# Reordering matmuls of two widths, bank reads against weight preparation, and a wider final norm, in a float32 Conformer layer with its MLP

## The chip, the cores and the metric

The kernel runs on one NeuronCore of one Trainium2 chip. The metric is device time in microseconds (us) of one execution, as the median over several runs. The names of the engines are those of the profile: PE is the matrix engine, PEld its loading of weights, DVE the vector engine, ACT the scalar engine, POOL the general engine GpSimd, and SP the engine whose queue issues most of the DMAs.

## The reference

One layer of a streaming encoder on 512 tokens of width 2048, all in float32: an RMS norm, a Conformer convolution module, a residual, a second RMS norm, a squared-ReLU MLP with hidden width 8192, a residual, and a last RMS norm.

```python
h = rmsnorm(x, norm1_g)
y = conformer_conv(h, ...)     # matmul 2048 -> 4096, sigmoid gate, 31-tap causal
                               # convolution, layernorm, silu, matmul 2048 -> 2048
x = x + y
h = rmsnorm(x, norm2_g)
x = x + square(relu(h @ mlp_w1)) @ mlp_w2
return rmsnorm(x, final_g)     # y = x * rsqrt(mean(x*x) + 1e-6) * g
```

## The kernel before, in words

**Float32 products from rounded halves.** Every factor is split into a high part `hi` in the rounded format (`fp32r`) and a low part `lo = x - hi`. A product is then high times high, plus the two cross terms. In the second half of the MLP, the convolution module and the last pieces these are three matmuls of 512 columns (`mm3`, L395 to L397). In the first half of the MLP the activations hold `hi` and `lo` of 256 tokens side by side in one tile `y` of 512 columns. One matmul of 512 columns with the high weights `wh` (L1114) serves two terms, and one of 256 columns with the low weights `wl` (L1115) the third.

**The MLP, first half.** It is computed by seven block products (`P1` to `P7`, a Strassen scheme on two by two blocks) for each of 32 pairs of hidden tiles (`n`, L1110). A product runs over eight `p`, each with a 512 and a 256 column matmul: 1792 of each in all. The order of products is `FIRST = P1, P5, P6, P2, P7, P3, P4`. They accumulate in PSUM banks: `P1`, `P6`, `P7`, `P4` in bank X (bank 0 or 1, alternating with `n`), `P5` and `P3` in Y, `P2` in Z. A bank is read after each product that it held, into a block of the tile `four`: by an ACT copy and a DVE add (L1122, L1123), or by two DVE adds (L1120, L1123). The next product in the bank has to wait for that read.

**The weights.** `stream` is one list of all weight chunks. `emit()` prepares the next: DMA from HBM (on SP), a sum of blocks where the scheme wants one, the cast to `wh` on ACT and the subtraction to `wl` on POOL or DVE. `chunk()` (L337) takes the next chunk and first emits up to `AHEAD` further ones. Each engine works through its queue in order, so where `chunk()` stands in the program decides what each engine's queue holds ahead of the bank reads.

**The beginning of the MLP.** The output projection of the convolution module runs in four quarters `q` of eight chunks `c` (L969). The last chunks, 6 and 7 of the last quarter, are multiplied at L990 to L996, one output tile after the other, and the evacuated tiles 12 to 15 are scaled and summed into the last two `p` of `y` (`y_sums`, `pieces`). `ahead()` makes two sums of weight blocks on POOL (`t5`, `t6`, L242). For the first pair (`n` = 0) the loop does more: further `pieces`, and `residual` transposes 12 to 15 on PE into banks that are free, whose reading (`residual_read`: ACT copies, squares and DMA) is placed by the tables `RESIDUAL` and `READ_FIRST`.

**The MLP, second half.** `seven()` (L1197) runs the same scheme for groups `g` of eight hidden tiles and two halves `q` of the columns. The last group has 14 products of twelve matmuls. `add` (L1194) reads each bank on DVE into the residual tiles `acc`. A last part without the scheme adds 512 hidden units directly.

**The final norm.** `Row` (L1256) treats 128 tokens: `piece` runs six matmuls of 512 columns and adds the bank to `acc` (DVE), squares it with a sum (ACT, L1274) and multiplies by `final_g` (POOL, L1279). `total` and `factor` turn the sums into the factor `r` (L1283 to L1291), which `scale` applies (L1296 on ACT, L1298 on DVE) ahead of the output DMA. The norm of one row stands between the pieces of the next. The last piece of the last row is cut in two of 256 columns.

## Time and profile before

| | us |
|---|---|
| median of 3 runs (lowest, highest) | 1849.67 (1848.84, 1849.75) |
| the profiled execution | 1847.88 |
| its span, first to last instruction | 1846.1 |
| PE busy | 1813.8 (98%) |
| DVE, POOL, ACT busy | 1308.6, 1254.6, 1168.1 |

The profile is one execution. Its span leaves out 1.8 us of the execution's own time. Matmuls overlap: the duration of one reaches past the start of the next, so what a matmul costs in a stream is read from one start to the next. "Idle before" is the time that an engine stood still ahead of an instruction, with what released it. POOL and DMA issue rows read in the same way.

### The profile page before, as it was taken

How to read it: one execution, taken by the hardware profiler on the slowest of the kernel's cores; microseconds unless marked ns; L12 is line 12 of the kernel's file. 1: busy time of each engine (PE TensorE's matmuls, PEld its weight loads, DVE VectorE, ACT ScalarE, POOL GpSimd, SP SyncE). 2: the span in 40 equal slices, each digit the busy share in tenths (PEclk: the TensorE clock that was granted, in tenths of full speed). 3: DMA queues.
4: the chain of work that ended last, by engine and by line, in shares of the span. 5: the costliest groups of instructions: out<-in, count | busy, mean ns of one | idle time of the engine just before them, and what ended most of it. 6: DMA issues, size and time to landing. Idle time of an engine off the chain costs nothing.

```text
span 1846.1 us, 25990 instructions
## 1 busy us (share of the span) xinstructions
PE 1813.8 (98%) x9096; PEld 1535.6 (83%) x9096; DVE 1308.6 (71%) x2200; ACT 1168.1 (63%) x1789; POOL 1254.6 (68%) x717
## 2 busy tenths in 40 slices
PE   8999999999998999999999999999999999999996
PEld 6888888998886888888888888888888888888875
DVE  6899999973348767667667667656666576666676
ACT  7444444565355666666666666657777777777774
POOL 2899989944425667767767767766666767576655
PEclk9999999999999999999999999999999999999998
DMA  8333343116333555665665665594647447475332
GB/s 292 92 92 92 104 125 110 63 40 212 114 114 109 173 212 178 209 212 178 209 212 179 209 212 179 203 357 162 248 174 302 189 176 274 157 282 203 133 127 92
DMA packets 92003, 322.89 MB, mean 175 GB/s; under 512 B 10208, under 2 KB 11872, under 8 KB 91872
## 3 DMA queue, kind: packets, MB, share of 16 engines
q1 hardware_dynamic: 70992, 259.81, 41.1%
q10 hardware_dynamic: 20880, 61.42, 8.3%
q8 instruction: 72, 1.18, 0.3%
q14 instruction: 59, 0.48, 0.1%
HBM read 256.70 MB, written 64.49 MB: 174 GB/s over the span
## 4 chain that ended last, share of the span: by engine, by line
PE 86%; DVE 10%; ACT 2%; issue 1%; DMA 0%; ACTq 0%; SPq 0%; DVEq 0%
PE mm L1114 23%; PE mm L396 14%; PE mm L395 14%; PE mm L397 14%; PE mm L1115 11%; PE mm L778 8%; DVE ax L479 4%; DVE y L924 1%; PE mm L996 1%; DVE acc L1194 0%; DVE ysums L913 0%; DVE ol L582 0%; PE ax L932 0%; DVE ax L667 0%; DVE ax L475 0%
## 5 line engine op out<-in xcount | busy, mean ns | idle before, releaser
L1114 PE MATMUL mm<-y,wh 128*128 128x512 f32 x1792 | 634.9, 399 | 3.2 <-DVE four L1123 3.2
L1115 PE MATMUL mm<-y,wl 128*128 128x256 f32 x1792 | 503.7, 281 | 0.0
L1114 PEld LDWEIGHTS mm<-y,wh 128*128 128x128 f32 x1792 | 337.3, 188 | 87.7 <-DVE four L1123 3.8
L251 POOL TENSOR_TENSOR wl<-b,wh 128x1024 fp32r<-128x1024 f32 x96 | 232.0, 2417 | 193.0 <-ACT wh L250 140.3
L219 DVE TENSOR_TENSOR wl<-b,ax 128x512 fp32r<-128x512 f32 x360 | 231.2, 684 | 172.3 <-ACT ax L218 132.1
L1115 PEld LDWEIGHTS mm<-y,wl 128*128 128x128 f32 x1792 | 339.1, 189 | 0.0
L395 PE MATMUL mm<-wh,ah 128*128 128x512 f32 x840 | 326.9, 389 | 1.2 <-DVE acc L1194 1.2
L397 PE MATMUL mm<-wh,al 128*128 128x512 f32 x840 | 326.8, 389 | 0.0
L396 PE MATMUL mm<-wl,ah 128*128 128x512 f32 x840 | 326.8, 389 | 0.0
L212 ACT CAST wh<-b 128x1024 fp32r<-128x1024 f32 x210 | 221.4, 1054 | 151.4 <-PE mm L397 149.7
L192 POOL TENSOR_TENSOR b<-b,b 128x1024 f32<-128x1024 f32 x120 | 286.7, 2411 | 44.1 <-DVE wl L219 30.3
L145 POOL TENSOR_TENSOR wl<-raw,wh 128x1024 fp32r<-128x1024 f32 x84 | 200.9, 2408 | 131.0 <-ACT wh L144 130.9
L479 DVE SCALAR_TENSOR_TENSOR ax<-u,v,ax 128x512 f32<-128x512 f32 x327 | 218.0, 748 | 0.0
L395 PE MATMUL mm<-xh,wh 128*128 128x512 f32 (+1 forms) x544 | 206.5, 380 | 5.3 <-ACT wh L144 5.2
L396 PE MATMUL mm<-xl,wh 128*128 128x512 f32 (+1 forms) x544 | 205.8, 378 | 1.0 <-DVE xl L389 1.0
L397 PE MATMUL mm<-xh,wl 128*128 128x512 f32 (+1 forms) x544 | 205.4, 378 | 0.0
L218 ACT COPY ax<-wh 128x512 f32<-128x512 f32 x360 | 199.8, 588 | 5.7
L1194 DVE SCALAR_TENSOR_TENSOR acc<-mm,shift,acc 128x512 f32<-128x512 f32 (+1 forms) x241 | 169.7, 742 | 31.0 <-PE mm L397 31.0
L395 PEld LDWEIGHTS mm<-wh,ah 128*128 128x128 f32 x840 | 157.7, 188 | 34.6 <-ACT w2h L1245 1.6
L397 PEld LDWEIGHTS mm<-wh,al 128*128 128x128 f32 x840 | 157.7, 188 | 32.6
L396 PEld LDWEIGHTS mm<-wl,ah 128*128 128x128 f32 x840 | 157.7, 188 | 32.6
L144 ACT CAST wh<-raw 128x1024 fp32r<-128x1024 f32 (+1 forms) x91 | 93.5, 1037 | 143.9 <-PE mm L396 99.1
(237 smaller groups left out, 2865.1 us busy)
## 6 DMA issues: line engine op xcount, KB each, us to landing
b<-in_w1s SPq DMA_DIRECT2D x128, 512.0 KB, 5.0
b<-in_w2s SPq DMA_DIRECT2D x120, 512.0 KB, 6.4
raw<-in_w_in SPq DMA_DIRECT2D x63, 512.0 KB, 3.8
ah<-spill SPq DMA_DIRECT2D x26, 896.0 KB, 8.4
al<-spill SPq DMA_DIRECT2D x26, 896.0 KB, 9.8
raw<-in_w_out SPq DMA_DIRECT2D x32, 512.0 KB, 3.6
spill<-sh ACTq DMA_DIRECT2D x31, 512.0 KB, 7.5
spill<-sl ACTq DMA_DIRECT2D x31, 512.0 KB, 7.5
```

Of the source, the lines that this page charges most:

```text
L145: (nc.vector if sl.stop == cut else self.eng).tensor_tensor(out=lo[:, sl], in0=raw[:, sl], in1=hi[:, sl].bitcast(F32), op=ALU.subtract)
L192: nc.gpsimd.tensor_tensor(out=raw[to, hs], in0=raw[x, hs], in1=raw[y, hs], op=ALU.subtract)
L212: nc.scalar.copy(out=hi, in_=self.s)
L218: nc.scalar.copy(out=st, in_=hi[:, sl].bitcast(F32))
L219: nc.vector.tensor_tensor(out=lo[:, sl], in0=self.s[:, sl], in1=st, op=ALU.subtract)
L251: nc.gpsimd.tensor_tensor(out=lo, in0=raw[b], in1=hi.bitcast(F32), op=ALU.subtract)
L395: nc.tensor.matmul(out=ps, lhsT=wh, rhs=xh, start=first, stop=False, **how)
L396: nc.tensor.matmul(out=ps, lhsT=wh, rhs=xl, start=False, stop=False, **how)
L397: nc.tensor.matmul(out=ps, lhsT=wl, rhs=xh, start=False, stop=last, **how)
L479: nc.vector.scalar_tensor_tensor(out=o, in0=a, scalar=w, in1=c, op0=ALU.mult, op1=ALU.add)
L1114: nc.tensor.matmul(out=x, lhsT=wh, rhs=t, start=product in OPENS and p == 0, stop=p == 7, skip_group_check=True)
L1115: nc.tensor.matmul(out=x[:, :HT], lhsT=wl, rhs=t[:, :HT], start=False, stop=p == 7, skip_group_check=True)
```

## The change

**Order of column steps.** Each product of the MLP's first half issues its eight 512 column matmuls first, then its eight 256 column ones. Nothing is added or left out.

PE, at the first product of the pair `n` = 0 (the row ahead of it belongs to the output projection). Before:

```order
L996 MATMUL mm<-vl,wh 128x512
L1114 MATMUL mm<-y,wh 128x512
L1115 MATMUL mm<-y,wl 128x256
L1114 MATMUL mm<-y,wh 128x512
L1115 MATMUL mm<-y,wl 128x256
```

After, with the first three products and the transposes (`ident`) of the residual:

```order
L1008 MATMUL mm<-vl,wh 128x512
L1121 MATMUL mm<-y,wh 128x512 x8
L1123 MATMUL mm<-y,wl 128x256 x8
L1121 MATMUL mm<-y,wh 128x512 x8
L1123 MATMUL mm<-y,wl 128x256 x8
L937 MATMUL mm<-ident,xr_3950 128x128
L937 MATMUL mm<-ident,xr_3952 128x128
```

The widths no longer alternate, and the first transposes have moved from behind the first product to behind the second.

**Bank reads ahead of weights.** For `n` = 0 and in the last group, the product takes a chunk that is already prepared (`chunk_made`), and the next one is emitted (`stream.get`) behind the bank's read. The sums and pieces for `P6` move from ahead of the loop to behind the first read, `P4`'s last piece goes earlier, and the residual's first two steps move from behind products 0 and 2 to behind 1 and 3. `residual_read` writes the squares back into their bank, and two reads share one tile.

DVE, from the last evacuation of the output projection (`xr15`) to the first two bank reads of `n` = 0 (`four`). `ysums` and `y` are the activations' sums and pieces, `ax` is a block sum for the weights of a later product. Before:

```order
L950 SCALAR_TENSOR_TENSOR xr15_3974<-mm_4781,v_91,xr15_3974 128x512
L913 TENSOR_TENSOR ysums_5234<-xs_5147 128x256
L924 TENSOR_TENSOR y_5236<-ysums_5234,y_5236 128x256
L913 TENSOR_TENSOR ysums_5234<-ysums_5234,xs_5147 128x256
L924 TENSOR_TENSOR y_5240<-ysums_5188,y_5240 128x256
L924 TENSOR_TENSOR y_5243<-ysums_5234,y_5243 128x256
L261 TENSOR_TENSOR ax_5144<-t6_5150,b11_4969 128x512
L261 TENSOR_TENSOR ax_5145<-t6_5150,b11_4969 128x512
L1123 TENSOR_TENSOR four_5304<-mm_5278,four_5304 128x256
```

After:

```order
L959 SCALAR_TENSOR_TENSOR xr15_3974<-mm_4781,v_91,xr15_3974 128x512
L918 TENSOR_TENSOR ysums_5234<-xs_5145 128x256
L929 TENSOR_TENSOR y_5236<-ysums_5234,y_5236 128x256
L1131 TENSOR_TENSOR four_5291<-mm_5271,four_5291 128x256
L918 TENSOR_TENSOR ysums_5234<-ysums_5234,xs_5145 128x256
L929 TENSOR_TENSOR y_5295<-ysums_5184,y_5295 128x256
L929 TENSOR_TENSOR y_5298<-ysums_5234,y_5298 128x256
L260 TENSOR_TENSOR ax_5142<-t6_5148,b11_5033 128x512
L260 TENSOR_TENSOR ax_5143<-t6_5148,b11_5033 128x512
```

The first bank read has moved ahead of five instructions.

**Chunks 5 to 7 of the last quarter.** Chunk 6's low part is made on DVE instead of POOL, and the loads of the MLP's first blocks are issued behind the DMAs of chunks 5 and 6.

SP, from the loads of the first pair's blocks (`b`) to the last chunk (`raw`). Before:

```order
L232 DMA b11_4969<-in_w1s 128x1024
L232 DMA b12_4971<-in_w1s 128x1024
L135 DMA raw_4975<-in_w_out 128x1024
L232 DMA b22_5031<-in_w1s 128x1024
L143 DMA raw_5035<-in_w_out 128x1024
L232 DMA b21_5084<-in_w1s 128x1024
L135 DMA raw_5088<-in_w_out 128x1024
```

After:

```order
L134 DMA raw_4971<-in_w_out 128x1024
L142 DMA raw_5029<-in_w_out 128x1024
L231 DMA b11_5033<-in_w1s 128x1024
L231 DMA b12_5035<-in_w1s 128x1024
L231 DMA b22_5037<-in_w1s 128x1024
L134 DMA raw_5086<-in_w_out 128x1024
L231 DMA b21_5150<-in_w1s 128x1024
```

Chunks 5 and 6 (`raw`) now pass the blocks `b11` to `b22`, and `b21` goes behind chunk 7.

**The final norm.** A row's squares are taken over 1024 columns, POOL multiplies only columns 0 to 1535 by `final_g` (of the last row 0 to 1023), and DVE applies `r` and `final_g` in one instruction to the rest. The last 512 entries of `final_g` lie in a PSUM bank (`g3`). The small instructions of `factor` become TENSOR_SCALAR with columns as scalars.

```diff
-                w = chunk()
+                w = chunk() if n else chunk_made()
                 for p in range(8):
-                    t = y[p, product]
-                    wh, wl = (h[:, p * P : (p + 1) * P] for h in w)
-                    nc.tensor.matmul(out=x, lhsT=wh, rhs=t, ...)
-                    nc.tensor.matmul(out=x[:, :HT], lhsT=wl, rhs=t[:, :HT], ...)
+                    nc.tensor.matmul(out=x, lhsT=w[0][:, p * P : (p + 1) * P], rhs=y[p, product], ...)
+                for p in range(8):
+                    nc.tensor.matmul(out=x[:, :HT], lhsT=w[1][:, p * P : (p + 1) * P], rhs=y[p, product][:, :HT], ...)
...
         for step, (product, hs) in enumerate(ORDER):
             if hs == halves:
                 continue
-            w = chunk()
+            w = chunk() if halves == 2 else chunk_made()
...
+            stream.get(cursor[0] - 1)
...
         def factor(self):
             nc.vector.reciprocal(out=y, in_=self.root)
-            nc.vector.scalar_tensor_tensor(out=ve, in0=y, scalar=ve, in1=y, op0=ALU.mult, op1=ALU.mult)
-            nc.vector.scalar_tensor_tensor(out=self.r, in0=ve, scalar=1.5, in1=y, op0=ALU.add, op1=ALU.mult)
+            nc.vector.tensor_scalar(out=ve, in0=y, scalar1=y, scalar2=ve, op0=ALU.mult, op1=ALU.mult)
+            nc.vector.tensor_scalar(out=self.r, in0=ve, scalar1=1.5, scalar2=y, op0=ALU.add, op1=ALU.mult)
...
+        g3 = bank("ax")
+        nc.scalar.copy(out=g3, in_=fgt[1][:, 512:])
...
+            row.piece(0, 512)
+            if before:
+                before.square(1024, 2048)
+                before.total()
+            row.piece(512, 1024)
+            if before:
+                before.gain(1024, 1536)
+                before.factor()
+            row.square(0, 1024)
+            if before:
+                before.scale(0, 1024, nc.scalar)
+            row.piece(1024, 1536)
+            if before:
+                before.scale(1536, 2048, nc.vector)
+                before.scale(1024, 1536, nc.scalar)
+            row.gain(0, 512)
+            row.gain(512, 1024)
```

More of the change, by code (lines that the diff above doesn't have):

```diff
@@ L319, in trunk @@
     for q in range(4):
-        items += [Plain(w_out[q, c], None if q == 3 and c in (5, 7) else nc.gpsimd) for c in range(0 if q else 4, 8)]
+        items += [Plain(w_out[q, c], (None if c in (5, 7) else nc.vector if c == 6 else nc.gpsimd) if q == 3 else nc.gpsimd) for c in range(0 if q else 4, 8)]
     AHEAD_AT = len(items) + 2
@@ L338, in chunk, with chunk_made @@
         got = stream.get(cursor[0])
+        cursor[0] += 1
+        return got
+    def chunk_made():
+        got = stream.made[cursor[0]]
         cursor[0] += 1
@@ L970, in trunk @@
             ps = [bank() for _ in range(4)]
-            stream.AHEAD = 3 if q < 3 else 2
+            stream.AHEAD, stream.LOAD = (3, 3) if q < 3 else (2, 0)
             for c in range(8 if q < 3 else 6):
                 w = chunk()
+                if q == 3 and c == 4:
+                    for x in items[cursor[0] + 3 :][:2]:
+                        x.load()
                 for i in range(2):
@@ L1138, in trunk @@
                 if n == 1 and i == 0:
+                    read = read()
                     gone.close()
@@ L1253, in trunk @@
         nc.scalar.dma_start(out=t, in_=fg[i * 1024 : (i + 1) * 1024].partition_broadcast(P))
-        fgt += [t[:, :512], t[:, 512:]]
+        fgt.append(t)
     class Row:
         def __init__(self, b):
-            self.b, self.xs = b, []
-            self.cols = [slice(n * 512, (n + 1) * 512) for n in range(4)]
-            if b == NTOK - 1:
-                self.cols[3:] = [slice(1536, 1792), slice(1792, D)]
+            self.b = b
             self.ss = tmp.tile([P, 5], F32, tag="st", name="ss")
-        def piece(self, i, cs):
-            b, n = self.b, cs.start // 512
-            ws = slice(cs.start - n * 512, cs.stop - n * 512)
-            ps = bank()[:, : cs.stop - cs.start]
+            self.sums = 0
@@ L1270, in piece, with square @@
+        def piece(self, start, stop):
+            b, n = self.b, start // 512
+            ws = slice(start - n * 512, stop - n * 512)
+            ps = bank()[:, : stop - start]
             for k in range(2):
                 mm3(ps, tuple(x[:, k * T + b * P :][:, :P] for x in a), tuple(x[:, k * 512 + ws.start : k * 512 + ws.stop] for x in wl2[n]), k == 0, k == 1)
-            x3 = add(b, n, ps, ws)
+            add(b, n, ps, ws)
+        def square(self, start, stop):
+            i = self.sums
+            self.sums += 1
@@ L1273, in piece @@
             sq = big.tile([P, 1024], F32, tag="rb", name="sq", bufs=8)
[L1274 to L1279 removed]
+            nc.scalar.activation(out=sq[:, : stop - start], in_=x2[self.b][:, start:stop], func=AF.Square, accum_out=self.ss[:, i : i + 1])
@@ L1281, in total, with gain @@
+        def gain(self, start, stop):
+            x3, i = x2[self.b][:, start:stop], start // 1024
+            nc.gpsimd.tensor_tensor(out=x3, in0=x3, in1=fgt[i][:, start - 1024 * i : stop - 1024 * i], op=ALU.mult)
         def total(self):
             self.t, self.root, self.y, self.ve, self.r = (tmp.tile([P, 1], F32, tag="st", name=f"r{i}") for i in range(5))
-            nc.vector.tensor_reduce(out=self.t, in_=self.ss[:, : len(self.xs)], axis=mybir.AxisListType.X, op=ALU.add)
+            nc.vector.tensor_reduce(out=self.t, in_=self.ss[:, : self.sums], axis=mybir.AxisListType.X, op=ALU.add)
@@ L1314, in trunk @@
             before = row
         before.total()
-        before.gain(i, nc.vector)
         before.factor()
-        for i in (4, 0, 3, 1, 2):
-            before.scale(i, i < 2)
+        for start, stop, eng in ((1792, 2048, nc.vector), (0, 512, nc.scalar), (1536, 1792, nc.vector), (1024, 1536, nc.vector), (512, 1024, nc.scalar)):
+            before.scale(start, stop, eng)
 def _c(a):
```

72 lines of the change are left out of this document (36 added, 36 removed).

## The prediction

> **What bounds the kernel now.** I read the page first, its busy times and the chain that ended last.
>
> ```profile
> PE 1813.8 (98%) x9096; PEld 1535.6 (83%) x9096; DVE 1308.6 (71%) x2200; ACT 1168.1 (63%) x1789; POOL 1254.6 (68%) x717
> PE 86%; DVE 10%; ACT 2%; issue 1%; DMA 0%; ACTq 0%; SPq 0%; DVEq 0%
> ```
>
> PE is the bound: only fewer matmul intervals, fewer waits of PE and the stretches without PE can be won. Next come stages, with the starts of PE's instructions in them.
>
> ```profile
> 700.00:900.00 200.00, 200.00 (x1134) 173.50 (x1133) 140.95 (x264) 133.94 (x214) 143.02 (x91) 1.00 0.58 200
> 1500.00:1770.00 270.00, 270.00 (x1193) 223.65 (x1192) 174.55 (x270) 198.33 (x269) 175.18 (x77) 1.00 0.52 196
> 556.98:601.91 44.93, 36.46 (x177) 30.04 (x176) 35.91 (x60) 28.81 (x65) 20.68 (x11) 0.92 0.36 112
> 1831.95:1846.10 14.15, 0.00 (x0) 0.00 (x0) 7.30 (x19) 5.80 (x16) 4.88 (x5) 0.62 0.51 185
> ```
>
> Columns: stretch, length, busy time and count of PE, PEld, DVE, ACT and POOL, granted clock, DMA share and GB/s. The first row lies in the MLP's first half, where widths alternate: PE never idles, and 200 us hold 567 pairs, 0.353 us each. No other engine is over 72% busy, so none is about to take over if a pair gets 2% shorter. The second row has 512 column matmuls alone: 270/1193 = 0.2263 us each (0.2267 without the partly covered ones at its ends). The third is the beginning of the MLP, with 8.5 us of idle PE and a mean clock of 0.92. The last is the tail without PE.
>
> PE's waits, from the timeline:
>
> ```profile
> 560.86 0.50 PE L996 MATMUL mm<-vh,wh 128*128 128x512 f32 x1 [2.36 <-ACT wh L136]
> 562.26 0.79 PE L996 MATMUL mm<-vh,wl 128*128 128x512 f32 x1 [0.90 <-DVE wl L140]
> 581.00 0.50 PE L1114 MATMUL mm<-y,wh 128*128 128x512 f32 x1 [1.62 <-DVE four L1123]
> 586.12 1.11 PE L932 MATMUL mm<-ident,xr 128*128 128x128 f32 x4 [2.03 <-ACT x L947]
> 592.65 0.50 PE L1114 MATMUL mm<-y,wh 128*128 128x512 f32 x1 [1.56 <-DVE four L1123]
> 1788.00 0.47 PE L395 MATMUL mm<-wh,ah 128*128 128x512 f32 x1 [1.25 <-DVE acc L1194]
> ```
>
> **Term 1, the order of widths.** A run of 256 column matmuls, each with its own weights, already stands in the last row's cut pieces:
>
> ```profile
> 1830.36 0.28 PE L395 MATMUL mm<-w2h,ah 128*128 128x256 f32 x1
> 1831.67 0.28 PE L397 MATMUL mm<-w2h,al 128*128 128x256 f32 x1
> ```
>
> These are the first and the last of twelve: 1.31/11 = 0.119 us from start to start, 0.120 when the first is left out. Eight and eight in runs cost 8 x 0.2267 + 8 x 0.120 = 2.774 us. At the two changes of width I add nothing, since in these rows the first 256 column matmul is as early as the others. Alternating, a product costs 8 x 0.353 = 2.825. The gain is 0.049 us a product. 217 products (pairs `n` 1 to 31) stand in the steady part: 10.6 us. The low weights are wanted 1.8 us later than before, the banks' reads come at the same point, and the deadline of a read (one product) shrinks by 2%, so I see no new wait there.
>
> [...]
>
> **Term 2, chunk 7 at 558 to 566.** Its casts come late because DVE is held up:
>
> ```profile
> 551.66 2.41 POOL L145 TENSOR_TENSOR wl<-raw,wh 128x1024 fp32r<-128x1024 f32 x1 [9.34 <-ACT wh L144]
> 551.92 7.50 DVE L924 TENSOR_TENSOR y<-xr,y 128x256 fp32r<-128x256 f32 x3 [0.39 <-ACT y L923]
> 559.76 1.04 ACT L136 CAST wh<-raw 128x1024 fp32r<-128x1024 f32 x1
> 562.20:565.60 3.40, 3.34 (x8) 2.67 (x9) 3.40 (x10) 3.40 (x9) 0.33 (x1) 0.51 0.00 0
> 586.10:589.10 3.00, 2.98 (x11) 2.69 (x12) 2.52 (x6) 3.00 (x8) 0.11 (x1) 0.50 0.95 354
> 551.11 0.41 DVE L924 TENSOR_TENSOR y<-ysums,y 128x256 fp32r<-128x256 f32 x1
> ```
>
> Three DVE instructions that take 0.41 us otherwise last 7.50: each sits out one of three POOL instructions in a row (chunk 6's low part, `t5`, `t6`). The change takes the first of these off POOL, and by SP's new order `t5` and `t6` find their blocks some 8 us earlier, behind chunk 4 instead of behind chunk 6. They then hold two DVE instructions (about 4 us instead of 7.50 - 3 x 0.41 = 6.3), and DVE has some 1.2 us more to do (two subtractions of 512 columns take 1.28 in term 4). Following the queues from there, an estimate, chunk 6's low part is ready near 555.7 (wanted near 557.2), and chunk 7's cast ends near 558.3 instead of 560.8; PE reaches it near 558.5 (560.86 less the wait). The wait of 2.36 us goes; what is late next is chunk 7's low part, which needs two more steps on ACT and DVE (1.4 us from the cast's end to PE's start at 562.26), so about 1.2 stays. With less idle time the half clock of the fourth row would not follow: 3.4 us at 0.51 cost 1.7. Lost there are 2.4 + 0.9 + 1.7 = 5.0, and some 1.3 stays: 3.7 us. The bounds: nothing, if DVE is held up just as long, and 5.0, if all of it goes.
>
> **Term 3, the pair `n` = 0.** The last four transposes and the start behind them give the price of a transpose:
>
> ```profile
> 601.56 0.60 PE L932 MATMUL mm<-ident,xr 128*128 128x128 f32 x4
> 601.91 0.48 PE L1114 MATMUL mm<-y,wh 128*128 128x512 f32 x1
> 580.86 4.02 DVE L924 TENSOR_TENSOR y<-xs,y 128x256 fp32r<-128x256 f32 x3
> 588.78 3.48 DVE L261 TENSOR_TENSOR mm<-b,t 128x512 f32<-128x512 f32 x2
> ```
>
> Four take 0.35. From 556.98 to 601.91 the matmuls need 48 x 0.227 + 7 x 2.825 + 4 x 0.35 = 32.1 us, so 12.8 of the 44.9 are lost: 5.0 in term 2, 7.8 here, 1.5 of that by half clock at 586 to 589. The read of the first bank now stands ahead of five DVE instructions, and P6 finds it in time: 1.62 us go. So do the 2.03: the transposes behind P6 waited for a bank, and now the first residual is read before the second is made. But DVE's work in between is the same, and so are POOL's `wl` subtractions, which hold it up (the last two rows). In runs the eighth 512 column matmul comes 1.6 us after the product's start instead of 2.5, so a piece of `y` is wanted 0.9 us earlier. Following the queues, an estimate again, I find 0.8 us of waits in P1 and P5, 1.4 in P2 (for the three `y` of the third row), and 1.8 and 1.6 in P7 (its bank, then its last piece, which stands behind the instructions of the fourth row): 5.6 in all, and four transposes fit into them. 7.8 - 5.6 + 0.35 + 0.3 (the order, six or seven products) comes to 2.85; I take 2.7, since a half clock may follow these waits too. Bounds of terms 2 and 3 together: 0 and 12.8.
>
> **Term 4, the last group.** The wait of 1.25 us (1.4 from start to start) is at the product behind P7, in the same bank. DVE did two low parts first:
>
> ```profile
> 1785.91 1.28 DVE L219 TENSOR_TENSOR wl<-b,ax 128x512 fp32r<-128x512 f32 x2
> 1787.11 1.40 DVE L1194 SCALAR_TENSOR_TENSOR acc<-mm,shift,acc 128x512 f32<-128x512 f32 x2
> ```
>
> With the read first it starts about 1.0 earlier (when its bank is done), and 0.4 stay: 1.0 us. Behind the read the low parts have two products of time, 5.4 us, for 2.5 us of DVE. The bounds are 0 and 1.4.
>
> **Term 5, the tail.** PE's last matmul ends at 1831.95, and DVE is then behind:
>
> ```profile
> 1831.88 0.74 DVE L1194 SCALAR_TENSOR_TENSOR acc<-mm,shift,acc 128x512 f32<-128x512 f32 x1
> 1832.94 0.94 DVE L1290 SCALAR_TENSOR_TENSOR r<-r,r 128x1 f32<-128x1 f32 x1
> 1833.91 1.18 DVE L1291 SCALAR_TENSOR_TENSOR r<-r,r 128x1 f32<-128x1 f32 x1
> 1838.04 0.40 ACT L1274 ACTIVATE sq<-acc 128x256 f32<-128x256 f32 x1
> 1838.35 0.18 ACT L1274 ACTIVATION_READ_ACCUMULATOR sq<-acc 128x1 f32 x1
> 1838.57 0.16 DVE L1283 TENSOR_REDUCE r<-ss 128x1 f32<-128x5 f32 x1 [1.24 <-ACT sq L1274]
> 1838.76 0.29 ACT L1284 ACTIVATE r<-r,eps_rms 128x1 f32<-128x1 f32 x1 [0.23 <-DVE r L1283]
> 1839.36 0.22 DVE L1290 SCALAR_TENSOR_TENSOR r<-r,r 128x1 f32<-128x1 f32 x1
> 1830.71 1.48 POOL L1279 TENSOR_TENSOR acc<-acc,fgt 128x512 f32<-128x512 f32 x1
> 1832.60 2.48 POOL L1279 TENSOR_TENSOR acc<-acc,fgt 128x512 f32<-128x512 f32 x2 [0.40 <-ACT sq L1274]
> 1831.80 0.15 DVE L1285 TENSOR_SCALAR r<-r 128x1 f32<-128x1 f32 x1
> L1034 ACT ACTIVATE four<-four 128x1024 f32<-128x1024 f32 x32 | 34.1, 1064 | 0.0
> L1296 ACT ACTIVATE acc<-acc,r 128x512 f32<-128x512 f32 x8 | 5.6, 709 | 0.8 <-DVE r L1291 0.8
> L1274 ACT ACTIVATE sq<-acc 128x512 f32<-128x512 f32 x15 | 9.5, 630 | 18.7 <-DVE acc L1194 18.0 <-DVE r L1283 0.7
> ```
>
> The last sum of squares starts 6.6 us after PE's end. The one-column SCALAR_TENSOR_TENSOR (STT) takes 0.94 and 1.18 us while POOL multiplies, and 0.22 without it; TENSOR_SCALAR beside POOL takes 0.15. Freed of that, DVE has four adds of 0.74, one wide STT like them and some 0.9 of small ones per row, 4.6 us against PE's 24 x 0.227 = 5.4, and keeps up. Then ACT decides. In the last row (18 x 0.227 + 12 x 0.12 = 5.5 us of PE, and 0.3 to the end of the last matmul) it has two squares of 1.06, a scaling of 1024 columns (about 1.1) and one of 0.71, squares of 0.63, 0.40 and 0.40, five accumulator reads of 0.18 and the root: 6.6 us, starting 1.0 after the row's first matmul and waiting some 1.0 for DVE in between. The last sum then starts 8.6 - 5.8 = 2.8 us after PE's end instead of 6.6. From there on the five scalings and DMAs leave at the queue's pace as now (0.1 more, since an STT takes longer than the TENSOR_SCALAR): 3.7 us. No row shows an STT with one operand in SBUF, a column and its third operand in PSUM; the nearest are the adds of L1194, one operand in PSUM, 0.74 beside POOL. If the new forms were held up like L1290, 1.8 us would stay: bounds 1.9 and 4.3.
>
> The Trainium skill, "SBUF — State Buffer", section "Who interferes with whom", says that a vector instruction with two SBUF inputs contends with a GpSimd instruction that reads SBUF, and one with a single SBUF input, outside the two-port modes, does not. By it the new forms run free, and the sum keeps 3.7; by the row of the replaced form (1.18) it would have 1.9. That TENSOR_SCALAR took 0.15 beside POOL agrees with the rule.
>
> **The sum.** 10.6 + 6.4 + 1.0 + 3.7 = 21.7 us. The profiled execution took 1847.88, 1.8 below the median; it would take 1826.2. Against the median of 1849.67 that is 1828.0.
>
> **Rivals.**
> 1. *Weight loads serialise in the runs of 256.* By the page's busy row a load lasts 1535.6/9096 = 0.169 us on the mean, longer than a 256 column interval. If eight in a row had to wait for their loads, a product would take 8 x 0.2267 + 8 x 0.169 = 3.17 us, and 224 of them 76 us more: 1915 with the other terms. It decides where a 256 column matmul passes 0.353 - 0.2267 = 0.126 us. Against it stand the runs at 0.119. Chance 0.04.
> 2. *The order is worth nothing*: this product's widths cost 0.353 a pair in runs as well, and the change does there not what it looks like. 21.7 less 10.6 and 0.3 leaves 10.8 us: 1838.9. For it speaks only that the runs seen so far are of other products. Chance 0.07.
> 3. *The waits at the MLP's beginning come back elsewhere*, since DVE and POOL are as busy there as before and pieces are wanted earlier: terms 2 and 3 give 1 instead of 6.4, and 1833.4 comes out. For it: DVE is busy 35.9 of 44.9 us. Chance 0.20.
> 4. *They all go*: 12 instead of 6.4, 1822.4. Against it the held-up `y` above. Chance 0.11.
>
> The forecast has the remaining 0.58.
>
> **How the numbers follow.** About 0.2% (3.7 us) is what a measurement of this kernel can tell from no change. Forecast and rivals 3, 4 and 2 are faster by more: 0.96, of which I take 0.02 for same, in case rivals 2 and 3 meet with a weaker tail. Faster 0.94, same 0.02, slower 0.04. The range goes from rival 4 to just beyond rival 3, which takes in terms 4 and 5 at their lower bounds beside the forecast: 1822.0 to 1834.5. It leaves out rivals 1 and 2 and the outer ends of the others, some 0.15 in all.
>
> **What the profile after would show.** In the steady part a product takes 2.774 us from first start to first start, 512 columns 0.227 and 256 columns 0.120. The wait for chunk 7's cast is gone and one for its low part is left, with no half clock near 562. Waits in the pair `n` = 0 sum to about 5.6 us, most of it at P2 and P7. The wait near the end of the last group is 0.4. The last sum starts about 3 us after PE's end, and no one-column instruction of the norm takes 0.9 us. A 256 column interval of 0.126 or more, or a new wait in every pair, would prove me wrong.

## The result, and the profile after

Six executions of the changed kernel took 1830.47 us in the median (1828.55 to 1831.20). Three further executions of the kernel before, beside it, took 1837.68, 1848.32 and 1837.87 us, so before has two times, which its first three executions (1848.84 to 1849.75) had not shown. The ratio to before is 0.9924, 95% interval 0.9894 to 0.9953: a gain of 0.76%, some 14 us of the 1848.58 that before took in the median of its six. The forecast was 1828.0/1849.67 = 0.9883, a gain of 21.7 us. The changed kernel came 2.5 us later than forecast, and before was not always at 1849.

The page of the profile after (span 1828.6, time 1830.43), busy times and chain:

```profile
PE 1806.1 (99%) x9096; PEld 1536.6 (84%) x9096; DVE 1302.4 (71%) x2197; ACT 1164.7 (64%) x1776; POOL 1247.2 (68%) x711
PE 88%; DVE 9%; ACT 2%; issue 1%; DMA 0%; SPq 0%; DVEq 0%; ACTq 0%
```

PE is still the bound. The windows by stage, first of before, then of after: chunks 6 and 7, the pair `n` = 0, pairs 1 to 31, the second half up to PE's end, the tail.

```profile
556.98:573.19 16.21, 12.95 (x49) 10.05 (x48) 11.40 (x20) 9.66 (x20) 8.53 (x5) 0.89 0.23 67
573.19:601.91 28.72, 23.51 (x129) 20.00 (x128) 24.51 (x41) 19.14 (x47) 12.14 (x6) 0.94 0.43 137
601.91:1215.39 613.48, 613.48 (x3476) 532.03 (x3474) 428.40 (x803) 408.72 (x651) 437.50 (x276) 1.00 0.57 200
1215.39:1831.95 616.56, 615.31 (x2720) 509.28 (x2718) 408.01 (x631) 442.06 (x611) 409.10 (x185) 1.00 0.54 203
1831.95:1846.10 14.15, 0.00 (x0) 0.00 (x0) 7.30 (x19) 5.80 (x16) 4.88 (x5) 0.62 0.51 185
```

```profile
557.16:569.07 11.91, 11.17 (x49) 8.93 (x48) 8.31 (x19) 9.53 (x20) 5.11 (x3) 1.00 0.10 40
569.07:596.89 27.82, 24.13 (x129) 20.04 (x128) 24.67 (x39) 17.39 (x43) 13.87 (x8) 0.94 0.51 161
596.89:1203.12 606.23, 606.23 (x3475) 533.53 (x3474) 428.52 (x804) 406.47 (x653) 438.34 (x276) 1.00 0.60 203
1203.12:1818.74 615.62, 615.36 (x2720) 509.12 (x2718) 408.14 (x635) 443.98 (x603) 405.66 (x183) 1.00 0.54 204
1818.74:1828.65 9.91, 0.00 (x1) 0.00 (x0) 3.30 (x11) 3.94 (x11) 1.83 (x2) 0.75 0.57 212
```

| stage | forecast gain, us | measured (difference of the rows) |
|---|---|---|
| chunks 6 and 7 (term 2) | 3.7 | 4.30 |
| the pair `n` = 0 (term 3) | 2.7 | 0.90 |
| pairs 1 to 31 (term 1) | 10.6 | 7.25 |
| second half (term 4) | 1.0 | 0.94 |
| tail (term 5) | 3.7 | 4.24 |
| start of the kernel | 0 | -0.18 |
| sum | 21.7 | 17.45 |

217 products in 606.23 us are 2.794 each: neither the 2.774 of the forecast nor the 2.827 (613.48/217) of before. PE's waits from 557 to 590, and the one of the last group, in the timeline after:

```profile
559.65 0.50 PE L1008 MATMUL mm<-vh,wl 128*128 128x512 f32 x1 [0.74 <-DVE wl L139]
574.35 0.50 PE L1121 MATMUL mm<-y,wh 128*128 128x512 f32 x1 [0.41 <-DVE y L929]
581.41 0.50 PE L1121 MATMUL mm<-y,wh 128*128 128x512 f32 x1 [0.75 <-DVE y L929]
583.95 1.88 PE L1121 MATMUL mm<-y,wh 128*128 128x512 f32 x7 [0.64 <-DVE four L1131]
587.66 0.50 PE L1121 MATMUL mm<-y,wh 128*128 128x512 f32 x1 [1.84 <-DVE y L929]
1774.77 0.47 PE L400 MATMUL mm<-wh,ah 128*128 128x512 f32 x1 [0.26 <-DVE acc L1210]
```

The wait for chunk 7's cast is gone, the waits for banks have shrunk to 0.64 and 0.26, and what is late now are pieces of `y`. Behind the longest of them comes half clock (window after):

```profile
587.70:590.95 3.25, 3.25 (x15) 3.11 (x15) 3.18 (x8) 2.81 (x8) 0.11 (x1) 0.55 0.66 190
```

### The profile page after: what moved, and what is told of

Same layout as the page of the kernel before. It is cut to its first block, busy times and chain, and to the rows that moved or that the text cites. A ratio compares the mean times of both kernels' runs of the same rounds, so it can differ in the third digit from the quotient of the medians.

```text
span 1828.6 us, 25981 instructions
## 1 busy us (share of the span) xinstructions
PE 1806.1 (99%) x9096; PEld 1536.6 (84%) x9096; DVE 1302.4 (71%) x2197; ACT 1164.7 (64%) x1776; POOL 1247.2 (68%) x711
## 3 DMA queue, kind: packets, MB, share of 16 engines
q8 instruction: 72, 1.18, 0.3%
## 4 chain that ended last, share of the span: by engine, by line
PE 88%; DVE 9%; ACT 2%; issue 1%; DMA 0%; SPq 0%; DVEq 0%; ACTq 0%
PE mm L1121 22%; PE mm L401 15%; PE mm L400 15%; PE mm L402 15%; PE mm L1123 12%; PE mm L783 8%; DVE ax L484 5%; DVE ysums L918 0%; DVE y L929 0%; PE mm L1008 0%; DVE ol L587 0%; PE ax L937 0%; DVE ax L672 0%; DVE ax L480 0%; ACT wh L143 0%
## 5 line engine op out<-in xcount | busy, mean ns | idle before, releaser
L1121 PE MATMUL mm<-y,wh 128*128 128x512 f32 x1792 | 450.6, 393 | 3.7 <-DVE y L929 3.0
L1121 PEld LDWEIGHTS mm<-y,wh 128*128 128x128 f32 x1792 | 322.7, 189 | 63.2 <-DVE y L929 4.7
L1123 PEld LDWEIGHTS mm<-y,wl 128*128 128x128 f32 x1792 | 245.1, 191 | 17.3
L1123 PE MATMUL mm<-y,wl 128*128 128x256 f32 x1792 | 250.6, 283 | 0.0
```

What stands on the lines that cost most here:

```text
L1121: nc.tensor.matmul(out=x, lhsT=w[0][:, p * P : (p + 1) * P], rhs=y[p, product], start=product in OPENS and p == 0, stop=False, skip_group_ ...
L1123: nc.tensor.matmul(out=x[:, :HT], lhsT=w[1][:, p * P : (p + 1) * P], rhs=y[p, product][:, :HT], start=False, stop=p == 7, skip_group_check ...
```

## The experiments

Each is the changed kernel with one edit, save the first two. "Product" is one of pairs 1 to 31 in that kernel's trace, in us.

| kernel | us: median (lowest to highest), executions | product |
|---|---|---|
| b_again (before) | 3 at 1837.15 to 1837.65, 9 at 1848.35 to 1850.15 | 2.827 |
| e_group | 1842.03 (1841.61 to 1843.54), 12 | 2.794 |
| e_alt | 3 at 1824.87 to 1825.62, 3 at 1836.01 to 1836.76 | 2.774 |
| e_run4 | 1832.37 (1832.08 to 1832.90), 4 | 2.807 |
| e_run2 | 1827.68 (1827.45 to 1828.15), 5 | 2.787 |
| e_kick | 1835.93 (1834.81 to 1836.45), 10 | 2.822 |
| e_kick2 | 1 at 1825.02, 11 at 1834.19 to 1837.29 | 2.821 |
| e_swap | 1835.52 (1833.91 to 1836.12), 10 | 2.820 |
| e_split128 | 1835.93 (1834.55 to 1836.87), 6 | both kinds |
| e_split256 | 1832.98 (1831.69 to 1833.38), 5 | both kinds |
| e_oldnorm | 1834.11 (1832.89 to 1835.34), 9 | 2.794 |
| e_wfirst | 1830.88 (1830.51 to 1831.13), 5 | 2.794 |
| e_c6pool | 1834.93 (1833.12 to 1836.07), 10 | 2.794 |
| e_gsb | 1830.44 (1829.87 to 1831.62), 10 | 2.794 |

**The two times of before: b_again** (no edit).

> The kernel before, unchanged. Its runs beside the changed kernel were 1848.3, 1837.7 and 1837.9 us, its runs ahead of the change all 1848.8 to 1849.8. Theory one: its time has two values, some 11.2 us apart, because the alternating pair of 512 and 256 columns costs 0.353 us in some executions and 0.3467 (0.2267 + 0.120, no extra for the change of width) in others: 1792 x 0.0063 = 11.2 us. Then a profile of a short execution shows 2.774 us a product in the MLP's first half and the same waits at 558 to 601 us as before. Theory two: the short executions lack the waits and the half clock at the MLP's beginning (12.8 us lost there in the profile of before): then the product stays at 2.825 and the span of 556.98 to 601.91 us shrinks to some 33. Either way the runs here fall into two groups near 1837.7 and 1849, and none lies between.

No execution lay between the groups, here or in the 95 others of before that ran ahead of the change and beside the kernels: of all 107, 36 took 1836.6 to 1838.9 us and 71 took 1847.8 to 1850.7. The profiled execution (1849.85) was a long one, with 2.827 a product. So this run confirms the two groups, not their cause.

**The order alone: e_group**, before with the new loop.

```diff
                 for p in range(8):
-                    t = y[p, product]
-                    wh, wl = (h[:, p * P : (p + 1) * P] for h in w)
-                    nc.tensor.matmul(out=x, lhsT=wh, rhs=t, ...)
-                    nc.tensor.matmul(out=x[:, :HT], lhsT=wl, rhs=t[:, :HT], ...)
+                    nc.tensor.matmul(out=x, lhsT=w[0][:, p * P : (p + 1) * P], rhs=y[p, product], ...)
+                for p in range(8):
+                    nc.tensor.matmul(out=x[:, :HT], lhsT=w[1][:, p * P : (p + 1) * P], rhs=y[p, product][:, :HT], ...)
```

> The kernel before with only the order of widths changed (eight of 512 columns, then eight of 256, per product). By the profile after, a product takes 2.793 us instead of 2.825: 224 x 0.032 = 7.2 us less than the long executions of before, so about 1842 us, with the waits at 558 to 601 us as they were. If pieces of y that are wanted 0.9 us earlier add waits to the first pair, 1 to 2 us of that are lost. Rival (theory one of the two values of before): it is 7 us faster than long executions of before and 4 us slower than short ones, since 2.793 lies between 2.825 and 2.774.

1842.03, one value: 7 us less than the long executions of before and 4 us more than the short ones, as the rival says. PE's waits in the pair `n` = 0:

```profile
581.73 2.11 PE L1112 MATMUL mm<-y,wh 128*128 128x512 f32 x8 [1.32 <-DVE four L1122]
593.36 3.69 PE L1112 MATMUL mm<-y,wh 128*128 128x512 f32 x8 [3.04 <-DVE four L1122]
```

P7's wait is 3.04 here and 1.56 in the profile of before, and the pair takes 30.36 us instead of 28.72. That is not the order's doing. In b_again, which has no edit, P7's wait is 3.05 too:

```profile
594.50 0.50 PE L1114 MATMUL mm<-y,wh 128*128 128x512 f32 x1 [3.05 <-DVE four L1123]
575.51:603.77 28.26, 22.02 (x130) 18.73 (x128) 24.04 (x40) 18.75 (x45) 12.08 (x6) 1.00 0.47 139
```

What differs is the clock. In b_again it is full over the whole pair, in the profile of before it is half ahead of P7's wait (586.1 to 589.1), in e_group behind it (the eight matmuls there last 3.69 us, those at 581.73 2.11). Of the 2.1 us between e_group and b_again, such a half clock costs 1.5 (e_oldnorm, below). The medians leave 0.1 for the order: e_group is 7.1 us below the long executions (median 1849.16), and 217 x 0.0333 is 7.2. So the loss of 1 to 2 us in the first pair did not come.

**The order put back: e_alt**, the changed kernel with before's loop.

```diff
                 for p in range(8):
-                    nc.tensor.matmul(out=x, lhsT=w[0][:, p * P : (p + 1) * P], rhs=y[p, product], ...)
-                for p in range(8):
-                    nc.tensor.matmul(out=x[:, :HT], lhsT=w[1][:, p * P : (p + 1) * P], rhs=y[p, product][:, :HT], ...)
+                    t = y[p, product]
+                    wh, wl = (h[:, p * P : (p + 1) * P] for h in w)
+                    nc.tensor.matmul(out=x, lhsT=wh, rhs=t, ...)
+                    nc.tensor.matmul(out=x[:, :HT], lhsT=wl, rhs=t[:, :HT], ...)
```

> The changed kernel with the alternating order of widths put back. If all else of the change is independent of the order, it takes 1830.4 + 217 x 0.032 = 1837.4 us, and what the order costs in the first pair shows as less waiting there (pieces of y wanted 0.9 us later). Theory one of the two values: in some executions it takes 1837.4 and in others 1826 to 1827 (pairs of 0.3467). Theory two: it has one value, since the waits of the MLP's beginning are no longer there to go.

Two groups again, 11 us apart, and this time the profile fell on a short execution (1825.22). The same window in it, and in after (that of before is in the prediction, 1134 matmuls):

```profile
700.00:900.00 200.00, 200.00 (x1156) 176.34 (x1155) 143.35 (x268) 136.84 (x219) 146.95 (x95) 1.00 0.61 203
```

```profile
700.00:900.00 200.00, 200.00 (x1147) 175.99 (x1146) 142.26 (x266) 134.67 (x217) 143.53 (x91) 1.00 0.59 199
```

200 us hold 578 alternating pairs, 0.346 us each, against 0.353 in before: the same instructions in the same order at full clock, in two patterns. Theory one holds; theory two (waits that vanish) falls, since the difference lies in the pairs that never wait. The long executions of e_alt and the short ones of before have no profile: that they run in the other pattern is inferred from the 11 us, for which 217 x 0.053 = 11.5 is the estimate. Runs of eight lie between the two. So runs of eight gain 5.8 us against the long group (median 1836.26) and lose 5.2 against the short one (1825.22).

**Runs of four and of two: e_run4, e_run2.** The loops of e_run4, then that of e_run2. There and in the next group `k` is 0 for 512 columns with `wh` and 1 for 256 with `wl`:

```diff
+                for o in (0, 4):
+                    for p in range(o, o + 4):
+                        nc.tensor.matmul(out=x, lhsT=w[0][:, p * P : (p + 1) * P], rhs=y[p, product], ...)
+                    for p in range(o, o + 4):
+                        nc.tensor.matmul(out=x[:, :HT], lhsT=w[1][:, p * P : (p + 1) * P], rhs=y[p, product][:, :HT], ...)
...
+                for k, p in [(k, p + o) for p in range(0, 8, 2) for k in range(2) for o in range(2)]:
```

> The changed kernel with runs of four: four of 512, four of 256, four of 512, four of 256 columns per product. In the profile after, the first five 512 column matmuls behind a run of eight 256 take 0.234, 0.236, 0.228, 0.232 and 0.231 us instead of 0.227, together 0.027 more (0.019 net of an early first 256 column one). Theory one, a fixed cost of going back from a run of 256 to 512: two such returns per product give 2.774 + 2 x 0.019 = 2.812 us, 4.2 us longer than the changed kernel, 1834.6. Theory two, a debt that grows with the number of 256 column matmuls (weight loads that fall behind in the run and are caught up behind it): the same 0.019 per product, 2.793, and no difference to the changed kernel.

> The changed kernel with runs of two: 512, 512, 256, 256 columns, four times per product. Runs of eight cost 0.020 us per product over 8 x 0.2267 + 8 x 0.120 = 2.774, runs of four 0.033. Theory one, every return from 256 to 512 columns costs some 0.017 to 0.020 when it does not lock into the short pattern: four returns give 0.07 to 0.08 and 2.84 to 2.85 us a product, 1840 us. Theory two, what a return costs shrinks with the run before it, since only the last matmuls of a run are behind: at most 0.033 again, 2.807, 1832. If a pattern of two can lock as the alternation does, 2.774 and 1826 come out in some executions.

Runs of eight lose 0.020 us a product against 2.774, runs of four 0.033, runs of two 0.013. For e_run4 the measured 2.807 lies nearer to a fixed cost of each return (2.812) than to theory two (2.793); e_run2 then falls far below the 2.84 of a fixed cost; a cost that shrinks with the run allows it, but eight lose less than four. Neither theory stands. What holds is that each of these orders has one pattern, and that runs of two, at 1827.68, beat both kernels (ratio to before 0.9903, 0.9871 to 0.9934; all five executions lie below all six of the changed kernel). Of the 2.8 us to the changed kernel the products give 1.4 (604.80 for 606.23 us); most of the rest is a half clock in the pair `n` = 0 that the profile of e_run2 does not have (26.19 for 27.82 us).

**What chooses the pattern: e_kick, e_kick2, e_swap, e_split128, e_split256.** The first two put one product per pair in runs and alternate in the other six; the third shifts the alternation by one in each product; the last two cut one matmul per pair in two. The loops, in this order (`RUN8`, `RUN2` and `ALT` stand for the lists of runs of eight, runs of two and the alternation):

```diff
+                for k, p in RUN8 if i == 0 else ALT:
+                for k, p in RUN2 if i == 0 else ALT:
+                for k, p in [(0, 0)] + [(k, p + 1 - k) for p in range(7) for k in range(2)] + [(1, 7)]:
+                        if n and i == 0 and p == n % 8 and k == 1:
+                            cut = [slice(0, 128), slice(128, 256)]
+                        if n and i == 0 and p == 1 + n % 7 and k == 0:
+                            cut = [slice(0, 256), slice(256, 512)]
```

> The changed kernel with the first product of each pair n in runs of eight and eight, the other six alternating. In the alternating order a product took 2.827 us in the profile of before and 2.774 in that of the changed kernel with the order put back, steadily through 31 pairs, and both values stand side by side in the first pair of before, where waits interrupt the stream. Theory one, the interval locks in one of two patterns when a stretch of alternation begins, by its phase, and keeps it until the stream is interrupted: each pair n locks anew behind its run, so the value may change from pair to pair within one execution (if the phase behind a run differs), or is the same in all 31 and in all executions (if a run leaves always the same phase). Six products at 2.774 or 2.827 and one at 2.793 give 1825.8 (always short) to 1835.8 (always long). Theory two, the value is a property of the whole execution, set at its start: two groups of times near 1826 and 1836, as without the runs, each with one value in all pairs.

> The changed kernel with the first product of each pair n in runs of two, the other six alternating. With runs of eight in that place all 31 pairs went into the long pattern behind the run (2.830 us a product, 1834.8 to 1836.5 us in ten executions), so a run leaves always the same phase. Theory one, the phase in which a stretch of alternation begins decides: behind a run that ends 256, 256 the alternation begins in the same way whatever the run's length, so it is long again in all pairs, 1835 to 1836 us. Theory two, what the run left behind decides (runs of two lost 0.013 us a product over the least, runs of eight 0.020, so they leave another state): the short pattern can follow, in all pairs, and then six products of 2.774 and one of 2.787 give 1825.5 us. In both the time has one value.

> The changed kernel with the alternating order shifted by one inside each product: 512, 512, 256, 512, 256 and so on to 256, 256. One run of two per product between stretches of seven alternations. Theory one, the runs set the phase and the stretch behind them is long, at 0.3533 a pair: some 2.81 to 2.83 us a product, 1834 to 1838 us. Theory two, two 512s in a row give the weight loads room and the stretch behind them is short: 2.774 to 2.787, 1825 to 1828 us. In both the time has one value, since each product starts its stretch anew.

> The changed kernel in the alternating order, where in the first product of each pair n from 1 on one 256 column matmul (at p = n modulo 8) is cut into two of 128 columns. The same is computed. A 128 column matmul takes 0.110 us here, so a cut costs some 0.10 us a pair, 3.2 us in all. Theory one, the pattern is drawn by the phase at each interruption of the alternation: then pairs of both kinds stand in one execution (2.774 and 2.827 us a product from one n to the next), or, if this interruption leads always to one, all 31 are alike from n = 1 or 2 on and the time has one value, 1828.4 (short) or 1839.5 (long). Theory two, the pattern belongs to the execution: all pairs alike, and executions in two groups, 11 us apart.

> The changed kernel in the alternating order, where in the first product of each pair n from 1 on one 512 column matmul (at p = 1 + n modulo 7) is cut into two of 256 columns, so that three or four of 256 follow one another. The same is computed; a cut costs some 0.01 us a pair, 0.3 in all. Theory one, drawn at each interruption: pairs of both kinds in one execution, or all alike and one value of the time; the runs of two and of eight ahead of an alternation led to the long pattern in nearly all executions, so long is likelier here, 1836 to 1837, and 1825 to 1826 if short. Theory two, a property of the execution: two groups 11 us apart.

Behind runs of eight all 31 pairs of the trace were long and the time had one value, which speaks against theory two of e_kick. Behind runs of two it was long in 11 executions of 12, so theory one of e_kick2 holds with one exception (1825.02). In e_swap the shifted stretches cost 2.820 a product, near the long pattern: its theory one. The cuts decide between the theories. Windows of e_split128 over six uncut products of the pairs 8, 9, 10 and 11:

```profile
736.34:752.98 16.64, 16.64 (x99) 14.68 (x97) 11.37 (x22) 11.61 (x19) 12.60 (x9) 1.00 0.52 175
755.86:772.50 16.64, 16.64 (x99) 14.55 (x98) 11.35 (x22) 11.59 (x19) 12.86 (x9) 1.00 0.54 175
775.40:792.36 16.96, 16.96 (x98) 14.71 (x97) 11.10 (x21) 11.30 (x19) 13.09 (x9) 1.00 0.55 174
795.30:812.25 16.95, 16.95 (x98) 14.71 (x97) 11.55 (x22) 11.80 (x19) 12.75 (x9) 1.00 0.56 177
```

Two pairs at 16.64/6 = 2.773 and two at 16.96/6 = 2.827, in one execution; in e_split256 it is the same for its pairs 8 and 9:

```profile
736.89:753.53 16.64, 16.64 (x99) 14.67 (x97) 11.35 (x22) 11.59 (x19) 12.64 (x9) 1.00 0.55 174
756.33:773.29 16.96, 16.96 (x99) 14.70 (x97) 11.54 (x22) 11.79 (x19) 13.21 (x9) 1.00 0.57 179
```

In each of the two traces 12 of the 31 pairs are short and 19 long. The pattern is set at each interruption of the alternation and kept until the next. In before nothing interrupts it behind `n` = 0, so what is set there holds for 217 products, and the time of the whole kernel has two values.

It is not set by lot. In the long pattern the spacing of the pairs repeats every three pairs: 0.36, 0.35 and 0.35 us. The last starts of `wh` ahead of two cuts of e_split256, with the cut (x2):

```profile
813.56 0.40 PE L1127 MATMUL mm<-y,wh 128*128 128x512 f32 x1
813.92 0.40 PE L1127 MATMUL mm<-y,wh 128*128 128x512 f32 x1
814.27 0.40 PE L1127 MATMUL mm<-y,wh 128*128 128x512 f32 x1
814.62 0.40 PE L1127 MATMUL mm<-y,wh 128*128 128x256 f32 x2
851.36 0.40 PE L1127 MATMUL mm<-y,wh 128*128 128x512 f32 x1
851.72 0.40 PE L1127 MATMUL mm<-y,wh 128*128 128x512 f32 x1
852.07 0.40 PE L1127 MATMUL mm<-y,wh 128*128 128x256 f32 x2
```

At 814.62 two spacings of 0.35 lie between the one of 0.36 and the cut, and the pairs behind are short; at 852.07 one does, and they are long. So it is in the whole trace (pairs 2 to 31): a cut with two such spacings ahead of it led to the short pattern 12 times of 12, one at the two other places of a long stretch to the long pattern 7 times of 7, and a cut in a short stretch to the long one 11 times of 11. In e_split128 the cut at one place of a long stretch led to the long pattern 9 times of 9, at the other two to the short one 10 times of 10, and in a short stretch to the long one 9 times of 11 (in the two others the short pairs were evenly spaced, in the nine alternately 0.343 and 0.350 apart). The place in the pattern at which the interruption falls decides what follows.

**Chunk 6: e_c6pool.**

```diff
-(None if c in (5, 7) else nc.vector if c == 6 else nc.gpsimd)
+(None if c in (5, 7) else nc.gpsimd)
```

> The changed kernel with chunk 6's low part made on GpSimd again, and nothing else undone. Theory one: what removed the wait of 2.36 us for chunk 7's cast is that no GpSimd instruction holds DVE at 552 to 559 us any more; in the profile after, the three y instructions there took 1.09 us, GpSimd being idle from 551.3 to 562.7. With one such instruction back, DVE is held some 2 us, chunk 7 comes 1 to 2 us later and the time is 1831.5 to 1833. Rival: it is the earlier place of the two block sums, in front of chunk 5, that freed DVE; then the low part on GpSimd takes work off DVE and costs nothing, 1830.4, or its own 2.4 us makes PE wait for it, where the profile shows the wait at the low part of chunk 6 and not at chunk 7.

The time rose by 4.5 us, more than either theory gave: chunks 6 and 7 take 17.55 us at a mean clock of 0.81, much as in b_again (17.36 at 0.80). DVE, POOL and PE in its timeline:

```profile
552.60 7.49 DVE L929 TENSOR_TENSOR y<-xr,y 128x256 fp32r<-128x256 f32 x3 [0.38 <-ACT y L928]
552.34 2.40 POOL L144 TENSOR_TENSOR wl<-raw,wh 128x1024 fp32r<-128x1024 f32 x1 [9.33 <-ACT wh L143]
554.69 2.59 POOL L241 TENSOR_TENSOR t<-b,b 128x1024 f32<-128x1024 f32 x1
557.35 2.45 POOL L241 TENSOR_TENSOR t<-b,t 128x1024 f32<-128x1024 f32 x1
561.52 0.49 PE L1008 MATMUL mm<-vh,wh 128*128 128x512 f32 x1 [2.32 <-ACT wh L135]
562.92 0.79 PE L1008 MATMUL mm<-vh,wl 128*128 128x512 f32 x1 [0.90 <-DVE wl L139]
```

These are before's 7.50, 2.36 and 0.90 again. The low part is queued in POOL ahead of the two block sums, which have to wait for it, and all three then fall on DVE's `y`. In the profile after, the sum `t6` had run at 548.82 and the three `y` took 1.09:

```profile
548.82 2.46 POOL L241 TENSOR_TENSOR t<-b,t 128x1024 f32<-128x1024 f32 x1
555.71 1.09 DVE L929 TENSOR_TENSOR y<-xr,y 128x256 fp32r<-128x256 f32 x3
```

**Reads ahead of weights: e_wfirst.**

```diff
-                w = chunk() if n else chunk_made()
+                w = chunk()
-                    stream.get(cursor[0] - 1)
-            w = chunk() if halves == 2 else chunk_made()
+            w = chunk()
-            stream.get(cursor[0] - 1)
```

> The changed kernel with the weights of a later product prepared ahead of the bank read again, in the first pair and in the last group. In the last group 1.0 us comes back (the wait of 1.25 instead of 0.26). In the first pair theory one says that the read's place is what removed 1.62 us at P6 and 1.56 at P7: two to four microseconds come back there, 1833.5 to 1835.5 us. Theory two: DVE's work between two reads is the same, so the waits only move to the pieces of y, and the first pair loses less than 1 us: 1831.5 to 1832.5.

Its last group, and its pair `n` = 0, in the timeline and a window:

```profile
1774.98 0.47 PE L400 MATMUL mm<-wh,ah 128*128 128x512 f32 x1 [1.25 <-DVE acc L1209]
```

```profile
569.49:596.11 26.62, 23.05 (x130) 18.59 (x128) 24.05 (x39) 18.16 (x45) 13.52 (x8) 1.00 0.52 168
```

The last group loses its 1.0 us again, exactly. The first pair does not: 26.62 us, without half clock, against 26.30 in e_oldnorm (below), which has the new place of the reads and no half clock either. Theory two holds: there the reads' place moves the waits and saves 0.3. The time, 1830.88, lies 0.6 below the range of that theory, which starts from the time of the changed kernel, whose profile has the half clock.

**The norm: e_oldnorm and e_gsb.**

The edit of e_oldnorm is the last part of the change's diff, from `fgt = []` to the last `scale`, undone. That of e_gsb:

```diff
-        g3 = bank("ax")
-        nc.scalar.copy(out=g3, in_=fgt[1][:, 512:])
+        g3 = fgt[1][:, 512:]
```

> The changed kernel with the final norm of before (squares of 512 columns, the gain on GpSimd, one-column scalar_tensor_tensor, no part of the weight in PSUM). By the two profiles the stretch behind PE's last matmul shrank from 14.15 to 9.91 us: theory one, all of that is the norm, and this kernel takes 1830.4 + 4.2 = 1834.6 us. Rival: part of it comes from elsewhere (PE ending in another phase against DVE's queue, the residual tiles as one), and less than 3 us come back.

> The changed kernel with the last 512 entries of the final weight read from SBUF instead of a PSUM bank, so that the wide scalar_tensor_tensor of the norm has two SBUF inputs. Theory one, such an instruction waits for GpSimd's multiplication beside it (as one-column ones took 0.94 and 1.18 us instead of 0.22 in the profile of before): the one of the last row but one, 0.74 us at 1818.02 in the profile after beside GpSimd's 1818.06 to 1820.57, takes 1.5 to 3 us, the two adds behind it come late, and the time is 0.5 to 1.8 us longer, 1831 to 1832.2 us. Rival: one operand's place makes no difference to it, 0.74 us again, and the time is 1830.4.

Windows of e_oldnorm, its pair `n` = 0, the stretch behind P7's wait for `y`, and its tail:

```profile
569.28:595.58 26.30, 22.58 (x130) 18.57 (x128) 22.85 (x36) 17.12 (x42) 13.89 (x8) 1.00 0.52 163
587.90:591.20 3.30, 3.29 (x20) 2.99 (x21) 3.23 (x8) 2.87 (x8) 0.11 (x1) 1.00 0.62 206
1817.45:1831.29 13.84, 0.00 (x0) 0.00 (x0) 7.29 (x18) 5.78 (x16) 4.86 (x5) 0.67 0.52 189
```

The tail is 13.84 instead of 9.91, 3.9 of the 4.24 us; the medians differ by 3.6, so theory one of e_oldnorm holds. The pair `n` = 0 has the same edits and the same wait as in the changed kernel, but this time PE kept its full clock behind it: 26.30 instead of 27.82, so the half clock costs 1.5 us. e_gsb, with the same wait (1.83), has the half clock again and takes 27.84. In e_gsb DVE and POOL stand so:

```profile
1817.59 0.74 DVE L1319 SCALAR_TENSOR_TENSOR acc<-acc,r,fgt 128x512 f32<-128x512 f32 x1
1817.71 2.98 POOL L1298 TENSOR_TENSOR acc<-acc,fgt 128x512 f32<-128x512 f32 x2 [0.68 <-ACT sq L1294]
```

Theory one falls: DVE was not held, the time did not change. But POOL, which came 0.12 us later, took 2.98 us. In the profile after:

```profile
1818.06 2.51 POOL L1298 TENSOR_TENSOR acc<-acc,fgt 128x512 f32<-128x512 f32 x2 [1.46 <-ACT sq L1294]
```

Here the instruction that started first went through and the other waited. The Trainium skill, "SBUF — State Buffer", section "Who interferes with whom", says that the order of issue decides who is blocked; this run agrees.

## Why the prediction was right or wrong

**Term 1 failed, and with it the comparison with before.** Two steps of it were wrong. The first is "At the two changes of width I add nothing": 0.020 us a product is lost there (2.794 - 2.774), at the return to 512 columns. In the profile after the eight 512 column matmuls behind a run of 256 take 1.84 us from the first start to that of the next run, for 8 x 0.2267 = 1.81:

```profile
803.68 2.00 PE L1121 MATMUL mm<-y,wh 128*128 128x512 f32 x8
805.52 0.76 PE L1123 MATMUL mm<-y,wl 128*128 128x256 f32 x5
```

The rows of the last pieces, on which the step rested, were the end of a stream, with no 512 column matmul behind the run. Over 217 products that is 4.3 us. The term came out at 7.25 and not at 10.6 - 4.3 = 6.3, since a product of before took 2.827; the forecast wrote 2.825, but its gain of 0.049 goes with 2.823. Neither sign that the prediction named for being wrong came, since the loss stands in the 512 column matmuls.

The second is "Alternating, a product costs 8 x 0.353 = 2.825", a price from one window of one execution. It is that of one of two patterns. In 36 of 107 executions before takes 1837.7 us (median), which goes with 2.774 a product. Against those the order loses 217 x 0.020 = 4.3 us; the changed kernel is still 7.2 us faster, through terms 2 to 5. That is why the ratio, 0.9924, is nearer to 1 than 1830.47/1849.67 = 0.9896.

The sum is short by 4.25 us (17.45 for 21.7): term 1 by 3.35 and term 3 by 1.8, while terms 2 and 5 gave 1.1 more than forecast. That the time came within 2.5 us of 1828.0 is in part luck, since these errors have different signs.

The trace of before held the warning. This window covers P4's eight pairs of the pair `n` = 0, which end where the transposes at 601.56 begin:

```profile
598.78:601.56 2.78, 2.78 (x19) 2.43 (x17) 2.75 (x6) 2.02 (x7) 0.00 (x0) 1.00 0.89 273
```

2.78 us for a product without runs, next to 2.827 on the mean from 601.91 on.

Rival 2 (the order worth nothing, 1838.9) was wrong for a long execution of before and too kind for a short one. The Trainium skill ("TensorE: Matmul & The Clock Gate", section "Back-to-back issue gap") gives N/2.4 + 2.5 ns for an isolated matmul and says that in a stream of weight loads and matmuls both set the spacing. An estimate by that formula is 0.325 us for a pair; no run here shows it: 0.227 and 0.120 in runs, and 0.3467 or 0.3533 alternating.

**Term 2 was right in kind and 0.6 small** (4.30 for 3.7; against b_again, whose chunks 6 and 7 take 17.36, the gain is 5.45). The forecast left two `y` instructions held by the block sums; those ran earlier than I had followed them, and nothing was held. e_c6pool shows that the new order of the loads without the other engine for the low part gains nothing; the other engine without the new order was not tried. The wait left for the low part of chunk 7 was 0.74, not 1.2, without half clock, as forecast.

**Term 3 was right in its waits and wrong in two sums.** Pieces of `y` are late in place of the banks, as rival 3 had it; of the waits forecast as 5.6 us, 3.6 came (P2 0.75 for 1.4, P7 0.64 and 1.84 for 1.8 and 1.6, 0.41 for 0.8 ahead of them). But a half clock of 1.5 us followed, of which the forecast had only a remnant. Without it (e_oldnorm) the pair is 2.4 us shorter than before, close to the 2.7, and 2.0 shorter than in b_again (28.26), which has no half clock there either. And the reason given was not the cause: with the weights ahead of the reads again the pair is only 0.3 longer. What else made it shorter (the transposes' place, `P6`'s pieces behind the first read, the squares in PSUM) was not tried apart.

**Terms 4 and 5 held:** 0.94 for 1.0, undone alone by e_wfirst; 4.24 for 3.7, of which e_oldnorm gives back 3.9. The last sum starts 1821.08 - 1818.74 = 2.3 us behind PE's end (2.8 forecast):

```profile
1821.08 0.16 DVE L1302 TENSOR_REDUCE r<-ss 128x1 f32<-128x4 f32 x1 [1.54 <-ACT sq L1294]
```

No small instruction of DVE is held any more. In the profile after those of `factor` run while POOL stands still; in e_gsb one runs beside POOL and takes 0.27, for the 0.94 of the form before:

```profile
1816.49 0.27 DVE L1309 TENSOR_SCALAR r<-r,r 128x1 f32<-128x1 f32 x1
1815.74 1.28 POOL L1298 TENSOR_TENSOR acc<-acc,fgt 128x512 f32<-128x512 f32 x1
```

But e_gsb also shows that the PSUM bank for the weight gains nothing: the time is the same without it.

**Open** is what in PE makes the two patterns and the cost of returning to 512 columns; no run shows it. Open too is what differs between the executions of before at the pair `n` = 0, where its pattern is set, since no short one of them has a profile.

## What to carry to other kernels

A steady stream of unequal matmuls can run in more than one pattern, with the same instructions and no wait in the profile: look for products of the same form at different speeds within one trace before a price from one window is multiplied by two hundred, and run the kernel before often enough to see whether its time has two values. An order whose pattern is fixed (runs of two here, 1827.68 us) can be worth more than one whose best is shorter (the alternation, 1824.87 at best, 1830.82 in the median). And an instruction on POOL can cost DVE more than its own time when it stands in the queue ahead of others: here it pushed two block sums onto DVE's critical work, 4.5 us for one subtraction.

## What the runs showed of the hardware that I had not expected

- Alternating 512 and 256 column matmuls, each with its own weights, take 0.3467 or 0.3533 us a pair. Which of the two follows from the place in the pattern at which the stream is interrupted, and it is kept for up to 613 us.
- Runs of one width cost 0.013 (two), 0.033 (four) and 0.020 us (eight) a product over the least, not in the order of their number of changes.
- The same wait of PE (1.84 and 1.85 us) was followed by 3.3 us at a clock of 0.55 in the changed kernel and by full clock in e_oldnorm, whose program is the same up to there, a difference of 1.5 us. The Trainium skill, "TensorE: Matmul & The Clock Gate", section "Part 1: The HAM clock gate", says that the window that decides is free-running and its effect varies from run to run; these two traces agree.
- With two SBUF inputs DVE, which had started 0.12 us earlier, held POOL (2.98 for 2.51 us), where before POOL had held DVE (0.94 and 1.18 us).
